# Attention operands issued in another order, and attention outputs stored as float32 and split where they are used

## The chip, the core and the metric

The kernel runs on one core of one Trainium2 chip. The metric is the time of one execution on the device in microseconds (us), the median of several runs. One core has five engines with queues of their own that run in order: TensorE (PE: matmuls, with its weight loads shown as PEld), VectorE (DVE), ScalarE (ACT), GpSimd (POOL) and SyncE (SP). In this kernel SP issues nearly all transfers between HBM and the on-chip memory (DMAs), which 16 DMA engines then carry out. Matmul results land in PSUM, in banks of 128x512 float32; VectorE and ScalarE read them from there.

## What is computed

One layer of a streaming encoder, 1024 positions of width 1024, in float32. Cut to the part around the change:

```python
h = rms_norm(x1, g_mix)
qa, ka, va, qb, kb, vb, ga, gb = split(h @ w_in)
oa = chunk_band_attention(norm(qa), norm(ka), va, rel_bias)
ob = diff_attention(rotary(norm(qb)), rotary(norm(kb)), vb, lam)
y  = sigmoid(ga) * (oa @ w_up_a) + sigmoid(gb) * (ob @ w_up_b)
x2 = x1 + y @ w_out
```

Attention A has 8 heads of 64: each query sees its own chunk of 64 positions and the 8 before it, with a learned bias by distance. Attention B has 4 heads, each with two softmax maps whose difference is applied. In front of this lies a gated feed-forward layer, behind it another and a last norm; the change touches neither.

## The kernel before

**Precision.** Every product is made of three: an operand is split into a high part (float32 rounded to `float32r`, a copy on ScalarE) and a low part (operand minus high part, a subtraction on VectorE), and `mm3` adds high x high, high x low and low x high. Weights are loaded raw (`w`), then split into `wh` (L211) and `wl` (L215). Three raw buffers and six split pairs circulate: a raw buffer is loaded again once its low part has been made.

**Order.** The program is written as one stream of PE instructions. Work of the other engines that follows a product is put into a *chain* (`pe.chain`): a list of steps, each with a delay in ns on a clock that counts PE's matmuls (`Lag.now`). A step is emitted when that clock has passed it, or at once when `settle` is called for one of the chain's keys. So the delays set where a step stands in its engine's queue, and no more; whether data are there is settled by semaphores when it runs. Tiles come from rings (`pe.tile(..., bufs)`): a ring of 2 gives the same memory again at every second call.

**Projections beside attention.** `filler` is a generator that makes the products of `h @ w_in`, one 128x512 result in eight steps of three matmuls. `steps(n)` draws n of them. Queries and keys are normed, transposed, split and stored (`qk_evac`), values split and stored (`v_evac`, L1218, staging ring `stg` of 2), gates stored (`g_evac`, L1228). Seven values' results are made ahead of attention A by `steps(7 * 8)`; the rest of the projections fills PE between the attention's own products.

**Attention A** (`PairA`, `run_a`). 8 heads of 4 pairs of 128-query blocks. Pair i's scores are made while pair i-1 is transposed and pair i-2 multiplied with the values. `prefetch` issues SP's loads: a head's keys `uk` (four DMAs, L1237) and bias (four, L1595) by `load(h)`; its queries in two halves of 512 (`uq`, ring of 2, two DMAs each, L1250) by `load_q(h, half)`; its values `uv` (L1300) by `load_v(h)`. Every second pair the 64x512 output is complete: it is added up in `olow`, split into `oT` (L1391, L1392), and both parts are stored to `o_d["a"]` (L1393).

**Attention B** (`ItemB`, `run_b`). 4 heads of 8 blocks. The normed output of a block is transposed, split into the two parts of `oT` (L1528, L1529), and after four blocks stored to `o_d["b"]` (L1532).

**Up-projection.** For each of two column halves c and each tile t of 128 positions there is a product "a" and a product "b" of 12 matmuls, "a" one tile ahead; `load_o` has loaded both parts of the attention's output for a tile, 512 KB in pieces of 512 bytes (L1632). The gates of a tile (`load_gates`, L1645, ring `xn` of 2 and one place more) go through a sigmoid (L1686) and are multiplied with the two products out of PSUM (L1691); the sum `y` (L1695) is transposed for the product with `w_out`, and frees the buffer for a later tile's gates. The product banks are a ring of 4 (`mm`) and one of 2 (`fill`), so six products can wait to be read.

Of the kernel before, what the change touches and what calls it, by code (L numbers as in the profile page):

```python
# [21 lines left out]
P = 128  # L22
# [232 lines left out]
def kernel(ctx, tc, io, out):  # L255
# [24 lines left out]
    qk_d = {n: dp.tile([P, 2, 4, S], F32, name=n + "_d") for n in ("qa", "ka", "qb", "kb")}  # L280
    v_d = {n: dp.tile([NT, P, 1024], F32, name=n + "_d") for n in ("va", "vb")}
    g_d = dp.tile([NT, P, 2, D], F32, name="g_d")
    o_d = {n: dp.tile([P, 2, 4, S], F32, name="o" + n + "_d") for n in "ab"}

    rope_d = dp.tile([P, 4 * NT * ROT], F32, name="rope_d")
    EW = 768
# [990 lines left out]
    class PairA:  # L1277
# [29 lines left out]
        def prefetch(self):  # L1307
            h, b = self.h, self.b
            self.load(h)
            self.load_q(h, b // 4)  # L1310
            self.load_v(h)
            if b == 2:
                self.load(h + 1)
            if b == 6:
                self.load_v(h + 1)
            if b % 4 == 2:
                self.load_q(h + b // 4, (b // 4 + 1) % 2)

        def score(self, i):
            sp = pools["sp"]  # L1320
# [41 lines left out]
        def values(self):  # L1362
            h, b = self.h, self.b
            v = self.v[h]
            pe.settle(self.ph)
            if b % 4 == 0:
                self.po[h, b // 4] = banks["o"]()
            po = self.po[h, b // 4]

            terms = [[], []]  # L1370
            for kb in range(self.k0, b + 2):
                at = [i for i, (_, k0, nk, _) in enumerate(self.p) if k0 <= kb < k0 + nk]
                for part in (self.ph, self.pl):
                    rhs = part[:, kb - self.k0, at[0] : at[-1] + 1, :]
                    terms[len(at) - 1].append((kb, at[0] + b % 4, at[-1] + 1 + b % 4, rhs))
            one, both = terms
            terms = both[:1] + one + both[1:]
            for i, (kb, q0, q1, rhs) in enumerate(terms):
                pe.matmul(
                    po[:, q0 * P : q1 * P], v[:, kb, :], rhs.rearrange("p a q -> p (a q)"),  # L1380
                    start=(i == 0), stop=(i == len(terms) - 1),
                )
            if b % 4 == 2:

                oT = pe.tile(ap, [P, 2, 512], F32R, "oT", 1)
                low = sp_tile([P, 512], "olow", 1)
                pe.chain(
                    (po, oT, low),
                    (340, lambda: nc.scalar.copy(low[:HD], po[HD:])),
                    (600, lambda: nc.vector.tensor_tensor(low[:HD], po[:HD], low[:HD], op=ALU.add)),  # L1390
                    (1090, lambda: nc.scalar.copy(oT[:HD, 0], low[:HD])),  # L1391
                    (1300, lambda: nc.vector.tensor_tensor(oT[:HD, 1], low[:HD], oT[:HD, 0].bitcast(F32), op=ALU.subtract)),  # L1392
                    (800, lambda: nc.sync.dma_start(  # L1393
                        o_d["a"][(h % 2) * HD : (h % 2 + 1) * HD, :, h // 2, (b - 2) * P : (b + 2) * P],
                        oT[:HD].bitcast(F32),
                    )),
                )

    def sp_tile(shape, tag, bufs):
        return pe.tile(pools["sp"], shape, F32, tag, bufs)  # L1400

    class ItemB:
# [114 lines left out]
        def finish(self):  # L1517
            h, b = self.h, self.b
            pe.settle(self.on)
            pt = banks["t"]()  # L1520
            pe.transpose(pt[:, :P], self.on, ident)
            if b % 4 == 3:
                self.oT[h, b // 4] = pe.tile(ap, [P, 2, 512], F32R, "oT", 1)
            oT = self.oT[h, b // 4]
            qs = slice((b % 4) * P, (b % 4 + 1) * P)
            pe.chain(
                (pt, self.on, oT),
                (88, lambda: nc.scalar.activation(oT[:, 0, qs], pt[:, :P], AF.Copy, scale=gsub)),  # L1528
                (350, lambda: nc.vector.scalar_tensor_tensor(  # L1529
                    oT[:, 1, qs], pt[:, :P], gsub, oT[:, 0, qs].bitcast(F32), op0=ALU.mult, op1=ALU.subtract  # L1530
                )),
                *([(420, lambda: nc.sync.dma_start(o_d["b"][:, :, h, b * P : (b + 4) * P], oT.bitcast(F32)))]  # L1532
                  if b % 4 == 0 else []),
            )

    def run_a(pairs):
# [67 lines left out]
    with tc.tile_pool(name="sa", bufs=1, reuse_waits="tile") as sp:  # L1604
        pools["sp"] = sp
        PairA.load(0)
        PairA.load_q(0, 0)
        steps(7 * 8)
        pe.poll(all=True)
        psum_stage("pp3", s=(1024, 1), t=(512, 3), o=(512, 1))  # L1610
        run_a([PairA(h, b) for h in range(8) for b in range(0, NT, 2)])
        pe.poll(all=True)
# [16 lines left out]
        oT["b", t] = fp.tile([P, 2, 4, P], F32R, name="ob", tag=f"e{t}")  # L1629

    def load_o(n, t):
        nc.sync.dma_start(  # L1632
            oT[n, t].bitcast(F32).rearrange("p a u s -> p (a u) s"),
            o_d[n][:, :, :, t * P : (t + 1) * P].rearrange("p a u s -> p (a u) s"),
        )

    gates, g2 = {}, []
# [6 lines left out]
                gates[c, t] = pe.tile(fp, [P, 2, 512], F32, "xn", 2)  # L1644
            nc.sync.dma_start(gates[c, t], g_d[t, :, :, c * 512 : (c + 1) * 512])  # L1645

    for t in range(4):
        load_o("a", t)
    load_gates(0, 0)
    for t in range(4):  # L1650
        load_o("b", t)
    for _ in filler:
        pass
    load_gates(0, 1)
# [6 lines left out]
    up = {}  # L1661

    def product(n, c, t):
        ps = up[n, c, t] = bank()
        o = oT[n, t]
        first = base_up + 4 * c + (0 if n == "a" else 2)
# [140 lines left out]
```

## Time and profile before

| | |
|---|---|
| median of 3 runs | 2191.67 us (2190.38 to 2193.26) |
| the profiled execution | 2190.83 us, span from first to last instruction 2189.1 us |
| PE busy | 2132.0 us, 97% of the span |
| VectorE, ScalarE, GpSimd busy | 1423.0, 861.7, 871.2 us |
| mean granted TensorE clock | 0.993 |
| DMA | 305.66 MB, mean 140 GB/s |
| attention A, attention B, up-projection begin at about | 822, 1012, 1340 us |

A busy PE says little about where time is lost; the waits do. A timeline row gives the start in us from the span's start, the length, the engine, the line and the instruction, and in brackets the idle time ahead of it and what ended that. For SP, several issues in a row are merged ("x4"), and their length includes time in which SP could not issue the next. The granted clock is the share of full speed at which PE was allowed to run in a stretch; its two levels are 2.4 GHz (1.00) and 1.2 GHz (0.50).

### The profile page before, as it was taken

To read this page: it belongs to the slowest core of one execution; us is meant where nothing else is said; L and a number is where in the kernel's file an instruction comes from. 1 tells how busy PE (TensorE), PEld (TensorE's weight loads), DVE (VectorE), ACT (ScalarE), POOL (GpSimd) and SP (SyncE) were. 2 spreads that over 40 slices of the span, in tenths; PEclk is the share of its full clock that TensorE was granted. 3 is DMA by queue.
4 is the path that set the end of the run, shared out by engine and by line. 5 is a ranking of instruction groups with operands and counts; after the bars stand their busy time and mean duration, and the time that the engine had idled before them with its cause. 6 is when DMAs were issued, how large, how long until landed. Compare 5 with 4: busy or idle time off the path is not lost.

```text
span 2189.1 us, 27974 instructions
## 1 busy us (share of the span) xinstructions
PE 2132.0 (97%) x10112; PEld 1777.7 (81%) x10112; DVE 1423.0 (65%) x2013; ACT 861.7 (39%) x1491; POOL 871.2 (40%) x775
## 2 busy tenths in 40 slices
PE   7999999999999998999999999899999999999998
PEld 6788888888877887887888888788788888888886
DVE  7767666677995435775666663433866566668698
ACT  5333223244334324664555553322433323235432
POOL 3645554453675314552111110000464544527375
PEclk9999999999999999999999999999999999999999
DMA  5234333376323456656543537632223333355531
GB/s 159 74 98 137 102 116 94 110 262 239 126 87 140 126 170 168 195 152 181 177 137 126 169 116 227 220 97 104 64 68 115 101 116 101 113 186 215 202 116 77
DMA packets 267602, 305.66 MB, mean 140 GB/s; under 512 B 17456, under 2 KB 177480, under 8 KB 267464
## 3 DMA queue, kind: packets, MB, share of 16 engines
q1 hardware_dynamic: 267320, 303.35, 43.4%
q8 instruction: 80, 1.31, 0.3%
q14 instruction: 58, 0.48, 0.1%
q0 software_dynamic: 144, 0.52, 0.1%
HBM read 210.21 MB, written 94.40 MB: 139 GB/s over the span
## 4 chain that ended last, share of the span: by engine, by line
PE 57%; DVE 5%; POOL 2%; DMA 2%; issue 2%; SPq 1%; ACT 1%; POOLq 0%; DVEq 0%; ACTq 0%
PE fill L90 28%; PE mm L90 20%; PE t L95 3%; PE s L90 3%; PE t L90 2%; DVE wl L215 2%; PE o L90 2%; SPq L1632 1%; POOL x L834 1%; DVE xTh L792 1%; DVE x L834 1%; DMA uq<-qa_d 0%; DMA xn<-g_d 0%; DVE acc L834 0%; POOL S L598 0%
## 5 line engine op out<-in xcount | busy, mean ns | idle before, releaser
L211 ACT CAST wh<-w 128x1024 fp32r<-128x1024 f32 (+1 forms) x228 | 201.3, 900 | 392.5 <-PE mm L90 130.1
L90 PE MATMUL fill<-wh,xTh 128*128 128x512 f32 x824 | 328.1, 405 | 3.4 <-DVE xTh L792 2.9
L215 DVE TENSOR_TENSOR wl<-w,wh 128x1024 fp32r<-128x1024 f32 (+1 forms) x227 | 293.7, 1308 | 37.2 <-ACT wh L211 36.5
L90 PE MATMUL fill<-wh,xTl 128*128 128x512 f32 x816 | 315.1, 393 | 0.0
L90 PE MATMUL fill<-wl,xTh 128*128 128x512 f32 x752 | 296.1, 394 | 0.0
L90 PE MATMUL mm<-xTl,wh 128*128 128x512 f32 (+1 forms) x572 | 220.4, 385 | 2.4 <-DVE xTl L616 1.8
L90 PE MATMUL mm<-xTh,wh 128*128 128x512 f32 (+1 forms) x572 | 221.1, 386 | 0.2 <-ACT xTh L450 0.2
L90 PE MATMUL mm<-xTh,wl 128*128 128x512 f32 (+1 forms) x572 | 220.1, 385 | 0.0
L90 PE MATMUL mm<-S,wh 128*128 128x512 f32 x640 | 197.0, 389 | 0.0
L90 PEld LDWEIGHTS fill<-wh,xTl 128*128 128x128 f32 x816 | 153.8, 189 | 33.2
L90 PEld LDWEIGHTS fill<-wh,xTh 128*128 128x128 f32 x824 | 155.5, 189 | 31.2 <-DVE xTh L792 3.3
L90 PEld LDWEIGHTS fill<-wl,xTh 128*128 128x128 f32 x752 | 142.3, 189 | 23.0
L90 PEld LDWEIGHTS mm<-S,wh 128*128 128x128 f32 x640 | 120.2, 188 | 24.9
L215 DVE TENSOR_TENSOR wl<-tw,wh 128x1024 fp32r<-128x1024 f32 x80 | 123.5, 1544 | 9.3 <-ACT wh L211 9.3
L90 PEld LDWEIGHTS mm<-xTl,wh 128*128 128x128 f32 x572 | 108.3, 189 | 24.5 <-DVE xTl L616 2.2
L457 POOL TENSOR_SCALAR rs<-ss 128x8 f32<-128x8 f32 (+1 forms) x56 | 11.5, 206 | 290.3 <-ACT xn L477 204.6
L90 PE MATMUL mm<-wh,xTh 128*128 128x512 f32 x376 | 126.6, 390 | 0.0
L90 PEld LDWEIGHTS mm<-xTh,wh 128*128 128x128 f32 x572 | 108.4, 189 | 21.6 <-ACT xTh L450 0.7
L90 PEld LDWEIGHTS mm<-xTh,wl 128*128 128x128 f32 x572 | 108.3, 189 | 21.2 <-POOL wl L215 0.2
L90 PE MATMUL mm<-S,wl 128*128 128x512 f32 x320 | 124.5, 389 | 0.0
L90 PE MATMUL mm<-wh,xTl 128*128 128x512 f32 x360 | 121.3, 389 | 0.0
L337 POOL TENSOR_TENSOR tw<-w,w 128x512 f32<-128x512 f32 x40 | 54.7, 1369 | 148.0 <-DVE wl L215 116.1
(259 smaller groups left out, 4846.5 us busy)
## 6 DMA issues: line engine op xcount, KB each, us to landing
w<-in_w_ffn_gu SPq DMA_DIRECT2D x88, 512.0 KB, 4.3
raw<-hq_d SPq DMA_DIRECT2D x70, 512.0 KB, 3.9
hq_d<-xn SPq DMA_DIRECT2D x98, 256.0 KB, 4.5
w<-in_w_ffn_down SPq DMA_DIRECT2D x44, 512.0 KB, 6.1
w<-in_w_in SPq DMA_DIRECT2D x40, 512.0 KB, 4.1
hq_d<-x SPq DMA_DIRECT2D x42, 256.0 KB, 4.2
x_d<-x SPq DMA_DIRECT2D x16, 512.0 KB, 3.2
uq<-qa_d SPq DMA_DIRECT2D x32, 256.0 KB, 5.1
```

Of the source, the lines that this page charges most:

```text
L90: self.nc.tensor.matmul(ps, lhs, rhs, **flags)
L95: self.nc.tensor.transpose(ps, x, ident)
L211: self.nc.scalar.copy(h, w)
L215: (lo_engine or self.nc.vector).tensor_tensor(l, w, h.bitcast(F32), op=ALU.subtract)
L337: nc.gpsimd.tensor_tensor(t[:, :512], u0, g0, op=ALU.subtract)
L457: nc.gpsimd.tensor_scalar(r, ss, 1.0 / n, EPS, op0=ALU.mult, op1=ALU.add)
L792: nc.vector.tensor_tensor(t[:, 1], raw, t[:, 0].bitcast(F32), op=ALU.subtract)
L834: return lambda: engine.tensor_tensor(to, by if by is not None else to, what, op=ALU.add)
L1632: nc.sync.dma_start(oT[n, t].bitcast(F32).rearrange("p a u s -> p (a u) s"), o_d[n][:, :, :, t * P : (t + 1) * P].rearrange("p a u s -> p ...
```

## The change

Three things are altered.

1. Ahead of attention A, the second half of head 0's queries and head 1's keys and bias are loaded after 16 of the 56 filler steps, not in the first pairs. Head 0's values are loaded at the second pair.
2. In `prefetch`, the next half head's queries are loaded ahead of the next head's keys and bias, and ahead of its values.
3. Attention outputs are stored as float32, not as two parts, in a layout by tile (`[P, NT, 4, P]`, so that what the up-projection loads for a tile is one run of 2 KB in each partition). `load_o` loads a tile into the place of its low part, and a chain splits it there: a copy on ScalarE into the high part, then a subtraction on VectorE in place. `product` settles that chain ahead of its first matmul. The loads for tiles 0 to 3 come in the order in which the products take them.

```diff
--- before.py
+++ after.py
@@ -280,7 +280,7 @@
     qk_d = {n: dp.tile([P, 2, 4, S], F32, name=n + "_d") for n in ("qa", "ka", "qb", "kb")}
     v_d = {n: dp.tile([NT, P, 1024], F32, name=n + "_d") for n in ("va", "vb")}
     g_d = dp.tile([NT, P, 2, D], F32, name="g_d")
-    o_d = {n: dp.tile([P, 2, 4, S], F32, name="o" + n + "_d") for n in "ab"}
+    o_d = {n: dp.tile([P, NT, 4, P], F32, name="o" + n + "_d") for n in "ab"}
 
     rope_d = dp.tile([P, 4 * NT * ROT], F32, name="rope_d")
     EW = 768
@@ -1308,13 +1308,14 @@
             h, b = self.h, self.b
             self.load(h)
             self.load_q(h, b // 4)
-            self.load_v(h)
+            if b % 4 == 2:
+                self.load_q(h + b // 4, (b // 4 + 1) % 2)
+            if b > 0:
+                self.load_v(h)
             if b == 2:
                 self.load(h + 1)
             if b == 6:
                 self.load_v(h + 1)
-            if b % 4 == 2:
-                self.load_q(h + b // 4, (b // 4 + 1) % 2)
 
         def score(self, i):
             sp = pools["sp"]
@@ -1382,17 +1383,15 @@
                 )
             if b % 4 == 2:
 
-                oT = pe.tile(ap, [P, 2, 512], F32R, "oT", 1)
-                low = sp_tile([P, 512], "olow", 1)
+                low = sp_tile([P, 512], "olow", 2)
+                t0 = b - 2
                 pe.chain(
-                    (po, oT, low),
+                    (po, low),
                     (340, lambda: nc.scalar.copy(low[:HD], po[HD:])),
                     (600, lambda: nc.vector.tensor_tensor(low[:HD], po[:HD], low[:HD], op=ALU.add)),
-                    (1090, lambda: nc.scalar.copy(oT[:HD, 0], low[:HD])),
-                    (1300, lambda: nc.vector.tensor_tensor(oT[:HD, 1], low[:HD], oT[:HD, 0].bitcast(F32), op=ALU.subtract)),
-                    (800, lambda: nc.sync.dma_start(
-                        o_d["a"][(h % 2) * HD : (h % 2 + 1) * HD, :, h // 2, (b - 2) * P : (b + 2) * P],
-                        oT[:HD].bitcast(F32),
+                    (1300, lambda: nc.sync.dma_start(
+                        o_d["a"][(h % 2) * HD : (h % 2 + 1) * HD, t0 : t0 + 4, h // 2, :],
+                        low[:HD].rearrange("p (t s) -> p t s", s=P),
                     )),
                 )
 
@@ -1520,17 +1519,15 @@
             pt = banks["t"]()
             pe.transpose(pt[:, :P], self.on, ident)
             if b % 4 == 3:
-                self.oT[h, b // 4] = pe.tile(ap, [P, 2, 512], F32R, "oT", 1)
+                self.oT[h, b // 4] = pe.tile(ap, [P, 512], F32, "oT", 2)
             oT = self.oT[h, b // 4]
             qs = slice((b % 4) * P, (b % 4 + 1) * P)
             pe.chain(
                 (pt, self.on, oT),
-                (88, lambda: nc.scalar.activation(oT[:, 0, qs], pt[:, :P], AF.Copy, scale=gsub)),
-                (350, lambda: nc.vector.scalar_tensor_tensor(
-                    oT[:, 1, qs], pt[:, :P], gsub, oT[:, 0, qs].bitcast(F32), op0=ALU.mult, op1=ALU.subtract
-                )),
-                *([(420, lambda: nc.sync.dma_start(o_d["b"][:, :, h, b * P : (b + 4) * P], oT.bitcast(F32)))]
-                  if b % 4 == 0 else []),
+                (88, lambda: nc.scalar.activation(oT[:, qs], pt[:, :P], AF.Copy, scale=gsub)),
+                *([(420, lambda: nc.sync.dma_start(
+                    o_d["b"][:, b : b + 4, h, :], oT.rearrange("p (t s) -> p t s", s=P)
+                ))] if b % 4 == 0 else []),
             )
 
     def run_a(pairs):
@@ -1605,7 +1602,10 @@
         pools["sp"] = sp
         PairA.load(0)
         PairA.load_q(0, 0)
-        steps(7 * 8)
+        steps(2 * 8)
+        PairA.load_q(0, 1)
+        PairA.load(1)
+        steps(5 * 8)
         pe.poll(all=True)
         psum_stage("pp3", s=(1024, 1), t=(512, 3), o=(512, 1))
         run_a([PairA(h, b) for h in range(8) for b in range(0, NT, 2)])
@@ -1629,9 +1629,15 @@
         oT["b", t] = fp.tile([P, 2, 4, P], F32R, name="ob", tag=f"e{t}")
 
     def load_o(n, t):
-        nc.sync.dma_start(
-            oT[n, t].bitcast(F32).rearrange("p a u s -> p (a u) s"),
-            o_d[n][:, :, :, t * P : (t + 1) * P].rearrange("p a u s -> p (a u) s"),
+
+        o = oT[n, t]
+        nc.sync.dma_start(o[:, 1].bitcast(F32), o_d[n][:, t])
+
+        need = 6300 if (n, t) == ("a", 0) else 9000 + 2720 * (2 * t - 1 if n == "a" else 2 * t + 2)
+        pe.chain(
+            (("o", n, t),),
+            (need - (15000 if t >= 4 else 0), lambda: nc.scalar.copy(o[:, 0], o[:, 1].bitcast(F32))),
+            (700, lambda: nc.vector.tensor_tensor(o[:, 1], o[:, 1].bitcast(F32), o[:, 0].bitcast(F32), op=ALU.subtract)),
         )
 
     gates, g2 = {}, []
@@ -1644,11 +1650,11 @@
                 gates[c, t] = pe.tile(fp, [P, 2, 512], F32, "xn", 2)
             nc.sync.dma_start(gates[c, t], g_d[t, :, :, c * 512 : (c + 1) * 512])
 
-    for t in range(4):
-        load_o("a", t)
+    for n, t in (("a", 0), ("a", 1), ("b", 0), ("a", 2)):
+        load_o(n, t)
     load_gates(0, 0)
-    for t in range(4):
-        load_o("b", t)
+    for n, t in (("b", 1), ("a", 3), ("b", 2), ("b", 3)):
+        load_o(n, t)
     for _ in filler:
         pass
     load_gates(0, 1)
@@ -1661,6 +1667,7 @@
     up = {}
 
     def product(n, c, t):
+        pe.settle(("o", n, t))
         ps = up[n, c, t] = bank()
         o = oT[n, t]
         first = base_up + 4 * c + (0 if n == "a" else 2)
```

**SP's queue from the first queries of attention A on, head 0** (`uq` queries, `uk` keys, `uv` values, `w_...` raw projection weights, `va_d` the stored values). Before:

```order
L1250 DMA uq<-qa_d 64x2x512 x2
L1218 DMA va_d<-stg 128x1024 x6
L174 DMA w_6383<-in_w_in 128x2x512
L174 DMA w_6402<-in_w_in 128x2x512
L1218 DMA va_d<-stg 128x1024
L174 DMA w_6410<-in_w_in 128x2x512
L174 DMA w_6416<-in_w_in 128x2x512
L1300 DMA uv<-va_d 128x8x128
L1237 DMA uk<-ka_d 64x512 x4
L1595 DMA bias<-e_d 32x576 x4
L1250 DMA uq<-qa_d 64x2x512 x2
L1300 DMA uv<-va_d 128x8x128
```

The same stretch of the changed kernel:

```order
L1250 DMA uq<-qa_d 64x2x512 x2
L1218 DMA va_d<-stg 128x1024
L1250 DMA uq<-qa_d 64x2x512 x2
L1237 DMA uk<-ka_d 64x512 x4
L1592 DMA bias<-e_d 32x576 x4
L1218 DMA va_d<-stg 128x1024 x5
L174 DMA w_6399<-in_w_in 128x2x512
L174 DMA w_6418<-in_w_in 128x2x512
L1218 DMA va_d<-stg 128x1024
L174 DMA w_6426<-in_w_in 128x2x512
L174 DMA w_6432<-in_w_in 128x2x512
L1300 DMA uv<-va_d 128x8x128
```

The second half's queries, and the next head's keys and bias, have moved from behind the values' load to behind the second store of values.

**SP's queue in head 5 of attention A**, at its second pair. Before:

```order
L1197 DMA kb_d<-stg 128x4x128 x2
L174 DMA w_8304<-in_w_in 128x2x512
L174 DMA w_8357<-in_w_in 128x2x512
L1237 DMA uk<-ka_d 64x512 x4
L1595 DMA bias<-e_d 32x576 x4
L1250 DMA uq<-qa_d 64x2x512 x2
L174 DMA w_8409<-in_w_in 128x2x512
```

The same stretch of the changed kernel:

```order
L1197 DMA kb_d<-stg 128x4x128 x2
L174 DMA w_8277<-in_w_in 128x2x512
L174 DMA w_8330<-in_w_in 128x2x512
L1250 DMA uq<-qa_d 64x2x512 x2
L1237 DMA uk<-ka_d 64x512 x4
L1592 DMA bias<-e_d 32x576 x4
L174 DMA w_8382<-in_w_in 128x2x512
```

The queries have passed the keys and the bias; the two weight loads still stand in front.

**VectorE's queue from the end of the projections into the up-projection** (`wl` low halves of weights, the fourth of them that of the fourth "a" up weight; L1698 multiplies a gate with a product; L1640 is the new subtraction). In the kernel before, only the rows without `oa` and `ob` are there. The changed kernel:

```order
L1640 TENSOR_TENSOR oa<-oa 128x512
L215 TENSOR_TENSOR wl<-w_11624,wh 128x1024
L1640 TENSOR_TENSOR oa<-oa 128x512
L215 TENSOR_TENSOR wl<-w_11666,wh 128x1024
L1640 TENSOR_TENSOR ob<-ob 128x512
L215 TENSOR_TENSOR wl<-w_11717,wh 128x1024
L1640 TENSOR_TENSOR oa<-oa 128x512
L215 TENSOR_TENSOR wl<-w_12225,wh 128x1024
L1698 TENSOR_TENSOR xn<-fill,xn 128x512
L1640 TENSOR_TENSOR ob<-ob 128x512
L1698 TENSOR_TENSOR xn<-mm,xn 128x512
L1702 TENSOR_TENSOR sg<-xn 128x512
```

The subtractions stand between the weights' low halves and the gate products; that of "b" tile 1 comes after the fourth low half and the first gate product. On ScalarE the new copies stand in the same way between the weights' high halves and the sigmoids.

## Rows read from the trace of the kernel before

**Rows 1.** Page part 1: busy us (share of the span) and instructions of each engine.

```profile
PE 2132.0 (97%) x10112; PEld 1777.7 (81%) x10112; DVE 1423.0 (65%) x2013; ACT 861.7 (39%) x1491; POOL 871.2 (40%) x775
```

**Rows 2.** Waits of PE: for what; us in total, times, longest us.

```profile
PE s L90 <- DMA uq<-qa_d: 10.6, 2, 6.4
...
PE mm L90 <- DVE xn L1691: 6.9, 1, 6.9
...
PE t L95 <- DVE p L1472: 1.2, 1, 1.2
...
PE t L95 <- DVE sg L1695: 0.6, 1, 0.6
```

**Rows 3.** Timeline of PE: start us, us, instruction, [idle before <-releaser].

```profile
840.22 1.51 PE L90 MATMUL s<-uk,uq 128*128 128x512 f32 x4 [6.35 <-DMA uq<-qa_d]
...
994.08 1.51 PE L90 MATMUL s<-uk,uq 128*128 128x512 f32 x4 [4.21 <-DMA uq<-qa_d]
...
1378.88 0.80 PE L90 MATMUL mm<-wh,oa 128*128 128x512 f32 x1 [6.92 <-DVE xn L1691]
```

**Rows 4.** Stretches: us, busy us PE, PEld, DVE, ACT, POOL, granted PE clock, DMA share, GB/s.

```profile
840.20:846.50 6.30, 6.28 (x21) 5.42 (x22) 1.55 (x4) 1.97 (x4) 0.80 (x1) 0.52 0.42 92
994.10:1000.30 6.20, 6.20 (x22) 5.32 (x23) 1.55 (x4) 1.91 (x4) 0.80 (x1) 0.54 0.50 177
1378.90:1382.30 3.40, 3.40 (x8) 2.66 (x9) 3.33 (x6) 0.63 (x1) 0.00 (x0) 0.52 0.22 69
...
1340.00:1372.00 32.00, 31.32 (x143) 25.31 (x141) 9.51 (x13) 8.05 (x9) 0.78 (x1) 1.00 1.06 313
```

**Rows 5.** Timeline of SP's queue, attention A, head 0.

```profile
828.13 0.37 SPq L1300 DMA_DIRECT2D uv<-va_d  x1
828.54 2.50 SPq L1237 DMA_DIRECT2D uk<-ka_d  x4
831.09 3.46 SPq L1595 DMA_DIRECT2D bias<-e_d  x4
834.70 1.18 SPq L1250 DMA_DIRECT2D uq<-qa_d  x2
```

**Rows 6.** DMA issues by line: count, KB each, median us from issue to landing.

```profile
uv<-va_d SPq DMA_DIRECT2D x8, 512.0 KB, 5.6
```

**Rows 7.** Timeline of SP's queue, attention A, head 5.

```profile
982.16 2.78 SPq L1237 DMA_DIRECT2D uk<-ka_d  x4
...
987.40 1.18 SPq L1250 DMA_DIRECT2D uq<-qa_d  x2
```

**Rows 8.** Timeline of ScalarE (ACT), up-projection.

```profile
1351.95 1.05 ACT L211 CAST wh<-w 128x1024 fp32r<-128x1024 f32 x1 [8.12 <-DMA w<-in_w_up_a]
...
1356.94 0.59 ACT L450 CAST xTh<-t 128x512 fp32r<-128x512 f32 x1 [2.59 <-PE t L95]
...
1377.05 1.06 ACT L1686 ACTIVATE xn<-xn 128x1024 f32<-128x1024 f32 x1 [14.05 <-DMA xn<-g_d]
```

**Rows 9.** Timeline of VectorE (DVE), end of the projections and up-projection.

```profile
1336.78 2.59 DVE L215 TENSOR_TENSOR wl<-w,wh 128x1024 fp32r<-128x1024 f32 x2 [9.88 <-ACT wh L211]
...
1355.50 0.69 DVE L1695 TENSOR_TENSOR sg<-xn 128x512 f32<-128x512 f32 x1
```

**Rows 10.** Timeline of SP's queue around the up-projection's start.

```profile
1327.65 6.58 SPq L1632 DMA_DIRECT2D oa<-oa_d  x4
...
1335.99 7.64 SPq L1632 DMA_DIRECT2D ob<-ob_d  x4
...
1368.29 0.73 SPq L1645 DMA_DIRECT2D xn<-g_d  x1
```

**Rows 11.** Timeline of SP's queue: a gate store from 128x512.

```profile
1323.99 0.32 SPq L1228 DMA_DIRECT2D g_d<-qn  x1
```

**Rows 12.** Timeline of PE: the first product with "b" tile 1.

```profile
1350.45 0.39 PE L90 MATMUL mm<-wh,ob 128*128 128x512 f32 x1
```

**Rows 13.** Stretch of one head in attention A; columns as in Rows 4.

```profile
850.19:879.50 29.31, 29.31 (x175) 25.48 (x174) 19.96 (x50) 16.54 (x39) 16.74 (x32) 1.00 0.57 149
```

## The prediction, made before the changed kernel was run

> **What bounds the kernel now.** First the page's busy times: TensorE (PE) has 97% of the span [rows 1], so only the time in which it stands still, or runs at a lower clock, is to be had. The list of what PE waited for says how much that is: two waits for the queries of attention A make 10.6 us, one for a product of the gates 6.9, one for a transposed gate product 0.6; no wait for VectorE in attention is above 1.2 [rows 2]. PE's timeline places the three long ones [rows 3]: 6.35 us in head 0 (first scores of block 4), 4.21 in head 5 (the same place), 6.92 in the up-projection, where a bank is not yet read out. The table by stretches adds what follows each: the granted clock is 0.52, 0.54 and 0.52 for 6.30, 6.20 and 3.40 us, close to the lower of the two levels [rows 4]. The stages between run without a stop. PE's instructions and their order are the same in both kernels; only their starts can move.
>
> **The change, part by part.**
>
> *A. Queries and keys of head 0.* Half 1 of head 0's queries is issued at 834.70, behind the values' load (828.13), which waits for the last store of va, and behind four key and four bias loads [rows 5]; the data come at 840.2, when PE has stood since 833.9 [rows 3]. Now these ten loads go out right behind va's second store, six stores sooner. Worth: 6.35 + 6.30 x (1 - 0.52) = 6.35 + 3.02 = 9.4 us. What is late next? The values: still issued at about 828.1, and the median of their loads is 5.6 us [rows 6], so they land at 833.7. Their first product stands behind four score matmuls (1.51 us at the low clock, half that at the high one [rows 3]), so PE wants them at about 834.6. That leaves 0.9 us, and the load now has the queue to itself, so I take 0, with a bound of 1 us. The price of the move: six stores of va stand behind ten more DMAs, which take SP 2.50 + 3.46 + 1.18 = 7.1 us [rows 5]. Their two staging buffers come free later and ScalarE waits for one; behind it stand only evacuations, and each bank is filled again four groups later (two tags of two banks): 0.
>
> *B. Every later half head.* The two query loads move ahead of four key and four bias loads: in head 5 from 987.40 to 982.16 [rows 7], 5.2 us against a wait of 4.21. Two weight loads still go out before them; what they may leave of the wait I put at 0, with a bound of 1 us. Worth: 4.21 + 6.20 x (1 - 0.54) = 4.21 + 2.85 = 7.1 us. Keys and bias go out 1.2 us later, for a head that starts three block pairs later: 0.
>
> *C. The up-projection.* PE waits there for a bank that the product with gate (0,3) has not read; VectorE waits for the sigmoid, ScalarE for the gate's load, 14.05 us [rows 8]. The gate's buffer was free when gate (0,0) had been added up, at 1355.50 + 0.69 = 1356.2 [rows 9], but SP issued the load at 1368.29 [rows 10]: it was busy with attention outputs, 6.58 us for four "a" tiles and 7.64 for four "b", so 1.65 to 1.9 each and 26 to 31 us for the 16. Each moves 1024 pieces of 512 bytes; now it moves half the bytes in 128 pieces of 2 KB. A DMA of that shape (a gate store, 128x512) takes SP 0.32 us [rows 11]; if time goes by bytes instead, half of 1.9 is 0.95. So all 16 take between 5 and 15 us, and SP is 11 to 26 us earlier; I take the nearer row, the same shape. Then gate (0,3) goes out by 1356.2, and even with the 8.8 us that it took here (1368.29 to the sigmoid's start at 1377.05) it is in by 1365.0, through the sigmoid by 1366.1 and multiplied by 1366.8, where PE stopped only at 1372.0. Worth: 6.92 + 3.40 x 0.48 = 8.55. The 0.6 at the first transposed gate product goes too, since the fourth "a" up weight, for which ScalarE waited 8.12 us [rows 8], is also issued sooner. Together 9.2 us.
>
> *D. The split moves.* Removed in attention: 16 casts and 16 subtractions in A, 32 subtractions in B. PE waits little for these engines there (1.2 us at most [rows 2]): a gain of 0 to 1, and I take 0. Added in the up-projection: 16 casts of 128x512 on ScalarE and 16 subtractions on VectorE; the nearest rows are 0.59 [rows 8] and 0.69 us [rows 9], 9.4 and 11.0 us beside an ScalarE busy 8.05 us in 32 and a VectorE busy 9.51 [rows 4]. They cost nothing as long as each ends before its product; without that cover, 16 x 1.28 = 20 us. The tightest is "b" 1: its split stands behind the high half of the fourth "a" up weight on ScalarE, its subtraction behind the low half. That weight's load can go out when the first raw buffer is read, at 1336.78 + 1.3 = 1338.1 [rows 9]. With 5.6 us [rows 6] it is in at 1343.7, with the 8.8 of C at 1346.9. Then cast 1.05, subtraction 1.3, gate product 0.69, split 0.69: done at 1347.4 or 1350.6, and PE wants it at 1350.45 [rows 12]. I take 0 (DMA has less to move now), with a bound of 1 us.
>
> *E. Stores.* Half the bytes, but in pieces of 512 bytes where attention had 2 KB. Only the first "b" load waits for one: it holds SP until the last store has landed. By the 5.6 us of rows 6, the largest near row, it leaves at about 1333 and is wanted two products (5.4 us) before "b" 1, at 1345: 0.
>
> **Sum.** 9.4 + 7.1 + 9.2 = 25.7 us. The profiled execution took 2190.8 us (span 2189.1), 0.8 below the median of the runs, 2191.67. So 2165.1 for that execution and **2166.0** for the median.
>
> **Rivals.**
> 1. *All three waits go*, as above: 2166, from 2165 to 2169 by the bounds in A to D.
> 2. *One wait comes back in another place.* In C: if the queue is not what held the gate, or the splits queue up behind the up weight, up to 9.2 us stay: 2175. For it: the DMA engines are full in that stretch (share 1.06 [rows 4]), so SP may have been slow because they were. Against: half the bytes halve that too. In A or B, values or queries 1 to 4 us late: 2167 to 2172. A page speaks for the first. The Trainium skill (DMA: Bandwidth & Descriptors, "Issuing engines are not separate DMA queues") says that the time a sequencer takes to initiate a DMA is usually small against the DMA itself. By that rule fewer pieces would free nothing on SP, and the time would be 2175; 6.58 us of SP for four loads [rows 10] speaks against it.
> 3. *The waits only shift.* VectorE or GpSimd becomes the bound of attention A once PE no longer stops, and 2188 to 2192 comes out. Against: a head's length without a wait runs with PE busy 29.31 of 29.31 us, VectorE 19.96 and GpSimd 16.74 [rows 13].
> 4. *Slower: split on demand.* ScalarE and VectorE take their instructions in order. If a cast waits for its load, or stands behind a late sigmoid, each split ends after its product is due: PE waits 16 times 1.28 us, 20 us, and, stopping before every product, stays at the lower clock for the pass: 192 matmuls of 0.425 us (3.40 us for 8 [rows 4]) instead of half that cost 41 more. With A and B gained, 2191.7 - 16.5 + 61 = 2236. It decides where splits end later than their products by more than the 0 to 3 us that D leaves; with a third of the products late it is 2195. Against: the loads start at 1327.65 [rows 10], and the first split is due four products before "b" 1, about 1339.6.
>
> **How the numbers follow.** Case 1 has 0.73, case 2 0.19, case 3 0.03, case 4 0.05. A measurement of this kernel can tell about 0.2%, 4.4 us, from no change; cases 1 and 2 lie beyond that, case 3 within it. Faster 0.92, same 0.03, slower 0.05. The range takes in case 1 with its bounds, 4 us more for small gains in attention that I put at 0, and case 2: 2161 to 2176, leaving out cases 3 and 4.
>
> **What would show it.** Right: no wait of PE for uq and none for the gate products above 1 us; the granted clock at 1.00 through attention A and the up-projection; the gate load (0,3) on SP right behind the first gate sum instead of 12 us after it; the 16 output loads in under 15 us of SP. Wrong: a wait for a split (oa, ob) or for uv in PE's list, a clock below 1 in these stages, or the same 10.6 us under another name.

## The result, and the profile after

The changed kernel takes 2164.22 us (median of 4 runs, 2162.68 to 2164.97) against 2191.18 for the kernel before on the same chip (4 runs, 2190.38 to 2193.26): a ratio of 0.9881 (95% interval 0.9869 to 0.9893), 27.0 us less. Forecast were 2166.0 and a range of 2161 to 2176. The time lies in the range, and what happened is the forecast's likeliest case: all three waits are gone. It is 0.8 us below the 2165 to 2169 that this case had by its own bounds, in the part of the range that was kept for small gains in attention. The profiled execution has a span of 2163.2 us, 25.9 less than before's 2189.1; the forecast's sum was 25.7.

PE has the same 10112 instructions. Of the 25.9 us, 19.6 are time in which it stood still (57.1 before, 37.5 now), and 6.3 are busy time, since fewer of its matmuls run at the lower clock (compare [rows 1]):

```profile
PE 2125.7 (98%) x10112; PEld 1773.4 (82%) x10112; DVE 1413.9 (65%) x1981; ACT 860.9 (40%) x1491; POOL 866.1 (40%) x775
```

32 VectorE instructions are gone: the 48 subtractions in attention less the 16 added in the up-projection. On ScalarE as many casts came as went.

What PE waits for between 815 and 1520 us (columns as in [rows 2]). The 10.6 for `uq`, the 6.9 for the gate product, the 0.6 for `sg` and the 1.2 for `p` are all gone, and no `oa`, `ob` or `uv` has come in. The 1.0 for `xTl` is not new: the kernel before has it at 1529.27, outside of this stretch.

```profile
PE s L90 <- DVE m L1337: 1.3, 1, 1.3
PE t L95 <- DVE xTl L451: 1.0, 1, 1.0
PE t L90 <- DVE pTl L1274: 0.7, 1, 0.7
PE o L90 <- DVE pTl L1274: 0.3, 1, 0.3
PE o L90 <- ACT pTh L1273: 0.2, 1, 0.2
PE s L90 <- DVE stg L1215: 0.2, 1, 0.2
```

PE's timeline at the places of [rows 3]: block 4's scores in head 0 and in head 5, and the first product of the up-projection. None has a bracket, so none was waited for, and four score matmuls take 0.80 us where they took 1.51 at the low clock:

```profile
834.43 0.80 PE L90 MATMUL s<-uk,uq 128*128 128x512 f32 x4
...
981.10 0.80 PE L90 MATMUL s<-uk,uq 128*128 128x512 f32 x4
...
1322.02 0.39 PE L90 MATMUL fill<-wh,oa 128*128 128x512 f32 x1
```

The stretches of the changed kernel (columns as in [rows 4]): attention A up to 1012 us, the rest of both attentions up to 1320, then a place in the feed-forward layer behind the up-projection, of which more below, and last the up-projection's start. The granted clock is at 1.00 in attention and at the up-projection's start, where [rows 4] had 0.52 to 0.54. The table ahead of the prediction lets attention B begin at about 1012 us, which is too early: attention A's last sum runs at 1074.59 in the kernel before and at 1058.72 in the changed one (rows under D).

```profile
822.00:1012.00 190.00, 188.48 (x1102) 162.62 (x1101) 126.25 (x312) 107.01 (x243) 94.76 (x176) 1.00 0.66 179
1012.00:1320.00 308.00, 306.79 (x1673) 262.65 (x1672) 181.99 (x421) 163.51 (x412) 35.78 (x76) 1.00 0.43 135
...
1528.90:1536.00 7.10, 7.07 (x28) 5.64 (x29) 6.94 (x16) 2.88 (x8) 0.00 (x0) 0.76 0.11 39
1320.00:1360.00 40.00, 40.00 (x186) 33.10 (x185) 26.13 (x39) 19.43 (x28) 0.78 (x1) 1.00 0.63 223
```

SP's queue in head 0 answers to [rows 5]. Queries, keys and bias go out 31 to 39 us sooner; the values go out when they did:

```profile
796.20 1.58 SPq L1250 DMA_DIRECT2D uq<-qa_d  x2
797.82 2.55 SPq L1237 DMA_DIRECT2D uk<-ka_d  x4
800.42 2.59 SPq L1592 DMA_DIRECT2D bias<-e_d  x4
...
828.64 0.37 SPq L1300 DMA_DIRECT2D uv<-va_d  x1
```

SP's queue at the up-projection answers to [rows 10]. Shown are the first and the last of the attention outputs' loads and gate (0,3), that is column half 0 and tile 3:

```profile
1309.52 1.42 SPq L1634 DMA_DIRECT2D oa<-oa_d  x2
...
1311.62 0.32 SPq L1634 DMA_DIRECT2D ob<-ob_d  x1
...
1328.90 0.32 SPq L1634 DMA_DIRECT2D ob<-ob_d  x1
...
1332.33 0.85 SPq L1651 DMA_DIRECT2D xn<-g_d  x1
```

The 16 loads have rows of 0.32 to 0.71 us each and 8.0 in all, where four of them took 6.58 and 7.64 before. VectorE's rows there: "b" 1's subtraction, and the first sum of the gates, which frees the buffer for gate (0,3):

```profile
1330.03 0.68 DVE L1640 TENSOR_TENSOR ob<-ob 128x512 fp32r<-128x512 f32 x1
...
1331.34 0.69 DVE L1702 TENSOR_TENSOR sg<-xn 128x512 f32<-128x512 f32 x1
```

The sum ends at 1332.0 and the gate's load leaves 0.3 us later, not 12.

To see where the 25.9 us come from, the span is divided at two points on PE: its first score of attention A, and its first product of the up-projection (1322.02 above; before: 1339.58).

| us | before | after | difference | forecast |
|---|---|---|---|---|
| up to the first score | 822.3 | 822.8 | +0.5 | 0 |
| both attentions | 517.3 | 499.2 | -18.1 | -16.5 (A, B) |
| up-projection to the end | 849.5 | 841.2 | -8.3 | -9.2 (C) |

The sum is right to 0.2 us, but with 1.6 more in attention and 0.9 less behind it; the experiments look for both. The 0.5 ahead of the first score is no more than what the executions differ by: it stands between 822.2 and 822.8 in the twelve that were profiled.

### The profile page after: what moved, and what is told of

It reads as the page before. It is cut to its first block, busy times and chain, and to the rows that moved or that the text cites. A ratio compares the mean times of both kernels' runs of the same rounds, so it can differ in the third digit from the quotient of the medians.

```text
span 2163.2 us, 27972 instructions
## 1 busy us (share of the span) xinstructions
PE 2125.7 (98%) x10112; PEld 1773.4 (82%) x10112; DVE 1413.9 (65%) x1981; ACT 860.9 (40%) x1491; POOL 866.1 (40%) x775
## 4 chain that ended last, share of the span: by engine, by line
PE 89%; DVE 5%; POOL 3%; issue 1%; ACT 1%; DMA 1%; POOLq 0%; DVEq 0%; ACTq 0%
PE mm L90 38%; PE fill L90 37%; PE t L90 5%; PE t L95 4%; PE s L90 3%; PE o L90 2%; DVE wl L215 1%; POOL S L598 1%; POOL S L600 1%; POOL S L599 1%; DMA w<-in_w_ffn_gu 1%; POOL x L834 0%; DVE xTl L616 0%; DVE xn L484 0%; DVE xTl L451 0%
```

## The experiments

Each kernel ran on one chip beside the kernel before; ratios are against that. The middle columns are the stages of the table above, from each kernel's profiled execution. The attention column moves also where an edit does not touch it (517.3 before, 511.1 and 510.9 in e4 and e5); the parts on A and B below say why.

| kernel | both attentions | rest | span | median us | ratio (95%) |
|---|---|---|---|---|---|
| e1: part 1 alone | 505.5 | 849.6 | 2177.5 | 2180.6 | 0.9961 (0.9949 to 0.9972) |
| e2: part 2 alone | 503.1 | 851.0 | 2176.9 | 2179.8 | 0.9959 (0.9946 to 0.9972) |
| e3: part 3 alone | 512.2 | 841.2 | 2176.0 | 2176.7 | 0.9944 (0.9932 to 0.9956) |
| e4: before, outputs laid out by tile | 511.1 | 839.5 | 2173.3 | 2179.4 | 0.9951 (0.9939 to 0.9963) |
| e5: before, four loads moved | 510.9 | 840.1 | 2173.7 | 2178.2 | 0.9950 (0.9937 to 0.9964) |
| e6: after, splits on demand | 499.0 | 849.1 | 2170.7 | 2173.9 | 0.9927 (0.9914 to 0.9939) |
| e7: after, old layout | 498.9 | 839.5 | 2160.9 | 2162.9 | 0.9879 (0.9865 to 0.9892) |
| e8: e4 with parts 1 and 2 | 500.9 | 839.5 | 2163.2 | 2164.9 | 0.9887 (0.9873 to 0.9902) |
| e9: after, again | 498.9 | 839.4 | 2160.5 | 2162.5 | 0.9877 (0.9860 to 0.9893) |
| e10: e7 again | 499.2 | 841.1 | 2162.9 | 2164.1 | 0.9883 (0.9869 to 0.9898) |

**e1, the early loads of head 0 alone.** The kernel before with

```diff
-            self.load_v(h)
+            if b > 0:
+                self.load_v(h)
...
-        steps(7 * 8)
+        steps(2 * 8)
+        PairA.load_q(0, 1)
+        PairA.load(1)
+        steps(5 * 8)
```

> The kernel before, with the first part of the change alone: head 0's second half of queries and head 1's keys and bias are loaded after 16 filler steps, and head 0's values at the second pair. Theory (what is lost is the wait and the lower clock behind it): PE's wait of 6.35 us in head 0 goes and with it the 3.0 us at half clock, the other two long waits stay as they are, 9.4 us less, a ratio of 0.9957. Rival 1 (only the wait counts): 6.4 us less. Rival 2 (the values are late next, or six delayed stores of values hold PE): a new wait for uv or stg in head 0 of 1 to 6 us, 3 to 8 us less.

Head 0 has no wait for queries, and none for values or the staging buffers has come in its place. Head 5 still waits; PE's timeline there, and the stretch behind it (columns as in [rows 4]):

```profile
983.57 0.87 PE L90 MATMUL s<-uk,uq 128*128 128x512 f32 x4 [2.93 <-DMA uq<-qa_d]
```

```profile
983.50:989.50 6.00, 5.93 (x27) 5.21 (x28) 2.19 (x5) 2.28 (x5) 0.80 (x1) 0.72 0.76 268
```

Attention is 11.8 us shorter. Head 5 cost 7.1 before and costs 2.93 + 6.00 x (1 - 0.72) = 4.6 here, through no part of the edit; so head 0's share is 11.8 - 2.5 = 9.3. The median fell by 7.7 us, between the 9.4 of the expectation and the 6.4 of its first rival: the rows tell the two apart, the time alone does not.

**e2, queries ahead of keys and bias, alone.** The kernel before with these lines moved up:

```diff
+            if b % 4 == 2:
+                self.load_q(h + b // 4, (b // 4 + 1) % 2)
             self.load_v(h)
...
-            if b % 4 == 2:
-                self.load_q(h + b // 4, (b // 4 + 1) % 2)
```

> The kernel before, with the second part alone: the next half head's queries ahead of the next head's keys, bias and values. Theory for head 5: its wait of 4.21 us goes with 2.9 us of half clock, 7.1 us less. In head 0 the queries then leave SP right behind the values' load, at about 828.6 in place of 834.7, and land some 5.4 us later at 834.0, when PE wants them at 833.9. So if the delay on SP is all there is, head 0 is cured as well, a wait of 1 us or less is left and the time falls by 15 to 16.5 us: then the first part of the change adds nothing to the second. Rival (each part cures its own head): head 0 still waits 3 us or more with the clock low after it, 7 to 9 us less in all.

Head 5's wait is gone. In head 0 this edit alone leaves little, for there too the queries now pass four key and four bias loads; PE's timeline:

```profile
836.29 0.87 PE L90 MATMUL s<-uk,uq 128*128 128x512 f32 x4 [1.48 <-DMA uq<-qa_d]
```

That lies between the two outcomes that were expected, 1 us or less and 3 us or more. After 1.48 us of waiting the clock stayed at 1.00. So parts 1 and 2 overlap: attention is 14.2 us shorter by part 2 alone and 11.8 by part 1 alone, and e8, with both, is only 2.2 below e2. The median fell by 8.4 us where the trace shows 12.2 less span; e2's six runs spread from 2175.8 to 2183.3, and the time alone would not have settled it.

**e3, the outputs alone.** The changed kernel with parts 1 and 2 undone.

> The changed kernel with the loads of attention A as before: only the third part (outputs stored as float32 by tile, split in the up-projection). Theory: the waits for queries stay at 6.35 and 4.21 us, the wait for gate (0,3) of 6.92 us, its 3.4 us at half clock and the 0.65 us wait go, 9.2 us less, a ratio of 0.9958. Rival (the gate's load was late for another reason than SP's queue, or the added splits cost): 0 to 4 us less.

The waits for queries stay, though shorter than before (5.54 and 2.66 us); the gate's wait, the one for `sg` and the one for `p` are gone. The rest is 8.3 us shorter, as in the changed kernel. Attention is 5.1 us shorter, which was not expected: the shorter waits (A and B below) and the moved split (D) make it up.

**e4, the layout without the format.** Both parts are still made in attention and stored, 512 KB a load, but by tile, so that a load is 128 pieces of 4 KB where it was 1024 of 512 bytes; a store is issued as two, one for each part (not shown here):

```diff
-    o_d = {n: dp.tile([P, 2, 4, S], F32, name="o" + n + "_d") for n in "ab"}
+    o_d = {n: dp.tile([P, NT, 2, 4, P], F32, name="o" + n + "_d") for n in "ab"}
...
-        nc.sync.dma_start(
-            oT[n, t].bitcast(F32).rearrange("p a u s -> p (a u) s"),
-            o_d[n][:, :, :, t * P : (t + 1) * P].rearrange("p a u s -> p (a u) s"),
-        )
+        nc.sync.dma_start(oT[n, t].bitcast(F32), o_d[n][:, t])
```

> The kernel before with the outputs still split in attention and stored as two parts, but in a layout by tile, so that a load of the up-projection is 512 KB in 128 pieces of 4 KB in place of 1024 of 512 bytes; each store is issued as two (one per part), 24 more. Nothing is split in the up-projection. Theory (SP's time for a load goes with its number of pieces): 0.3 to 0.6 us of SP per load in place of 1.65 to 1.9, the gate's load goes out by 1357, its wait goes, 9 us less, as much as with float32 outputs: the halved bytes and the moved split are not what pays. Rival (SP's time goes with the bytes, because the DMA engines are full): 1.5 us or more per load, the wait stays at 5 us or more, 0 to 3 us less.

SP's queue has the same bytes as [rows 10] in a third of the time:

```profile
1321.83 2.07 SPq L1634 DMA_DIRECT2D oa<-oa_d  x4
...
1324.70 2.35 SPq L1634 DMA_DIRECT2D ob<-ob_d  x4
```

The gate's wait is gone. The loads themselves are no faster: the medians from issue to landing are 7.8 ("a") and 10.0 us ("b"), 8.2 and 8.5 before. So the pieces set what a load costs SP, and SP's time is what the gate waited for.

**e5, the same loads at another place in the queue.** Nothing in the kernel before is changed but that tiles 6 and 7 are loaded behind gates (0,3) and (0,4):

```diff
-    for t in range(4, NT):
+    for t in range(4, 6):
...
             product("b", c, t)
+            if c == 0 and t in (1, 2):
+                for n in "ab":
+                    load_o(n, t + 5)
```

> The kernel before, with the loads of the last four attention outputs (a and b of tiles 6 and 7) moved behind the loads of gates (0,3) and (0,4) in SP's queue; the same DMAs with the same pieces and bytes. Theory (the gate's load stood in SP's queue behind loads that nobody needed yet): gate (0,3) leaves SP at about 1358 in place of 1368.29, PE's wait of 6.92 us and the half clock after it go, 7 to 9 us less with no change of layout or format. Rival (the DMA engines were full, and the gate's data come as late as before): the wait stays at 4 us or more, 0 to 3 us less. Third outcome: the moved loads come late themselves, a wait for oa or ob of tile 6.

Gate (0,3) leaves SP here, 19 us after the first product against 29 before:

```profile
1352.81 0.75 SPq L1645 DMA_DIRECT2D xn<-g_d  x1
```

PE has no wait for it, and the rest is 9.4 us shorter, with all the pieces and bytes of before. The median fell by 12.0 us, more than the 7 to 9 expected; in the profiled execution 6.4 us come from attention, which this edit does not touch. The 9.4 settle the cause of term C: it is the gate's place in SP's queue.

**e6, the cover of the splits taken away.** The changed kernel with each split emitted only when its product settles it:

```diff
-            (need - (15000 if t >= 4 else 0), lambda: nc.scalar.copy(o[:, 0], o[:, 1].bitcast(F32))),
+            (1e9, lambda: nc.scalar.copy(o[:, 0], o[:, 1].bitcast(F32))),
```

> The changed kernel with every output split emitted only when its product is about to be issued, not 3 to 6 us of PE work ahead. This is the cover under which the splits were costed at nothing. If each of the 16 products waits for its cast and subtraction: 16 times 1.28 us, and the lower clock for the pass, 20 to 61 us more than the changed kernel. If it is enough that ScalarE and VectorE reach the split while PE is still in the products emitted before it: waits of 1 us or less here and there, 0 to 5 us more.

Five products wait, all of them "b"; PE's list of waits:

```profile
PE mm L90 <- ACT ob L1639: 3.7, 3, 1.3
PE fill L90 <- ACT ob L1639: 2.9, 2, 1.7
```

Why "b" waits is seen on ScalarE, VectorE and PE at the longest of them. The cast of `ob` stands behind the sigmoid (second row; the gate's tile is called `gain` here), which stands behind a copy that waits for PE's own transposition of `y`; the cast of the next `oa` comes right behind it, a whole product ahead of its use. VectorE's subtraction for `ob` follows the cast:

```profile
1338.36 0.58 ACT L450 CAST xTh<-t 128x512 fp32r<-128x512 f32 x1 [8.06 <-PE t L95]
1338.85 1.06 ACT L1693 ACTIVATE gain<-gain 128x1024 f32<-128x1024 f32 x1
1339.80 0.61 ACT L1639 CAST ob<-ob 128x512 fp32r<-128x512 f32 x1
1340.31 0.62 ACT L1639 CAST oa<-oa 128x512 fp32r<-128x512 f32 x1
```

```profile
1340.44 0.69 DVE L1640 TENSOR_TENSOR ob<-ob 128x512 fp32r<-128x512 f32 x1 [3.37 <-ACT ob L1639]
```

```profile
1338.40 0.39 PE L90 MATMUL mm<-wh,oa 128*128 128x512 f32 x1
1340.46 0.50 PE L90 MATMUL fill<-wh,ob 128*128 128x512 f32 x1 [1.68 <-ACT ob L1639]
1340.80 0.40 PE L90 MATMUL fill<-wl,ob 128*128 128x512 f32 x1
1341.19 0.73 PE L90 MATMUL fill<-wh,ob 128*128 128x512 f32 x2
```

The clock stayed at 1.00. The rest is 9.7 us longer than in e9: 6.6 of waits, some 0.4 behind each stop, which makes 2.0, and about 1 that the rows do not explain. The 0.4 are lost over the first matmuls, which start 0.34 to 0.39 us apart and not 0.23; the third of them is the first to need the low part, and it starts when the subtraction has ended, at 1341.13. Neither expected outcome came: the loss is above the 0 to 5 us of the one and below the 20 to 61 of the other.

**e7, float32 in the old layout.** The changed kernel, but `o_d` is `[P, 4, S]`, so that a load has the same 256 KB in 512 pieces of 512 bytes (the stores follow):

```diff
-        nc.sync.dma_start(o[:, 1].bitcast(F32), o_d[n][:, t])
+        nc.sync.dma_start(o[:, 1].bitcast(F32), o_d[n][:, :, t * P : (t + 1) * P])
```

> The changed kernel with float32 outputs in the old layout, so that a load is 256 KB in 512 pieces of 512 bytes in place of 128 of 2 KB. By the number of pieces (or by the bytes) SP's time for a load is half of that before, 0.8 to 0.95 us, 15 us for 16: gate (0,3) still leaves SP some 10 us earlier than before, and the time is the changed kernel's within 1 us. Rival (the layout is needed): the wait for the gate comes back with 2 us or more, the time is 3 to 9 us above the changed kernel's.

SP takes 0.5 to 1.9 us a load, 14.6 in all. Two of its rows:

```profile
1308.81 2.26 SPq L1634 DMA_DIRECT2D oa<-oa_d  x2
...
1326.35 1.92 SPq L1634 DMA_DIRECT2D oa<-oa_d  x1
```

That is still early enough for the gate: no wait, and the time of the changed kernel.

**e8, everything but the format.** e4 with parts 1 and 2; the splits stay in attention.

> Both parts on the loads of attention A, and the layout by tile, but the outputs still split in attention and stored as two parts (as in the layout experiment): the change without its float32. Theory (the moved split gives back what VectorE held up at the seam between attention A and B): PE's wait of 1.2 us for the first transposes of B and some 0.3 us beside it are there again, from the first score to the up-projection 500.7 to 501.7 us in place of the changed kernel's 499.2, the up-projection as fast: 1.5 to 2.5 us above the changed kernel. Rival (the split's place is worth nothing): within 0.5 us of it and no such wait. It does not have the 16 copies and subtractions in the up-projection, so if those cost anything it gains that back there.

It is 2.4 us slower than e9 beside it (2164.90 against 2162.53; their runs don't overlap), and 2.0 of it are in attention: 500.9 against 498.9. One wait of [rows 2] is back:

```profile
1066.63 1.09 PE L95 MATMUL t<-ident,p 128*128 128x128 f32 x8 [1.23 <-DVE p L1473]
```

**e9 and e10, the changed kernel and e7 once more, side by side.**

> The changed kernel once more, beside the experiment without float32 on the same chip, so that the two can be set against each other: 25 to 28 us below the kernel before, and no wait above 1.5 us in attention A or the up-projection.

> Float32 outputs in the old layout once more, beside the changed kernel on the same chip: if the layout by tile is worth something, this is 1 us or more above the changed kernel; if fewer bytes are enough, the two are within 1 us.

e9 took 2162.5 and e10 2164.1; in the first runs it was 2164.2 and 2162.9. The order turned round, so the two layouts can't be told apart. In the profiled executions the slower of each pair is the one whose clock fell in front of the second feed-forward layer (C below). The fastest other version, e7 in its first runs, lies 1.3 us below the changed kernel, less than the 1.7 between the changed kernel's own two medians.

## Why the prediction was right, and where its terms were off

**What bounds the kernel.** Right: with PE's work unchanged, the time went by how long PE stood still and by the clock behind each stop.

**The sum, 25.7 us: measured 25.9, closer than its terms.** Attention gave 1.6 us more than forecast (D). The up-projection's start gave up to 10 where 9.2 were forecast (C), but 1.7 were lost again behind a wait that the change does not touch, and 0.5 ahead of the first score. In e9, the same kernel without that loss, the span is 2160.5. So the 0.2 is luck; that the time lies in the range is not.

**A, 9.4 us: measured 9.3** (e1, against the execution of before that the forecast read). Left alone, head 0 cost less in other kernels: in e3 a wait of 5.54 us and, by this row, 6.00 x (1 - 0.68) = 1.9 at the lower clock, 7.5 in all:

```profile
839.70:845.70 6.00, 5.98 (x27) 5.25 (x28) 2.04 (x5) 2.14 (x5) 0.81 (x1) 0.68 0.51 111
```

In e4 and e5 it was 7.6 and 7.1 (waits of 5.86 and 5.42 us, and a clock of 0.72 and 0.74 for 6.30). The values, feared late, were not: in the changed kernel they are issued at 828.64 and their first product runs at 835.07 without a wait. What the forecast missed is that its step B also reaches head 0: without A, only 1.48 us and some tenths would have been left there.

**B, 7.1 us: right for the execution that was read, and near the upper end of what comes up.** The same wait in kernels that leave head 5's order alone came out shorter, with and without a drop of the clock. PE's timeline and the stretch behind it in e3, and in e5, whose attention has the code of before:

```profile
991.00 1.51 PE L90 MATMUL s<-uk,uq 128*128 128x512 f32 x4 [2.66 <-DMA uq<-qa_d]
```

```profile
991.00:997.00 6.00, 6.00 (x19) 5.12 (x20) 1.56 (x4) 1.69 (x4) 0.80 (x1) 0.50 0.71 240
```

```profile
990.84 0.87 PE L90 MATMUL s<-uk,uq 128*128 128x512 f32 x4 [2.65 <-DMA uq<-qa_d]
```

```profile
990.80:997.00 6.20, 6.16 (x37) 5.46 (x38) 3.99 (x10) 3.65 (x8) 0.80 (x1) 1.00 0.81 283
```

With e1's 4.6, e4's 2.2, e3's 2.66 + 3.0 = 5.7 and e5's 2.65, term B lies between 2.2 and 7.1. The execution of before had the longest waits for queries of all that were profiled, in head 0 as in head 5. One profile of before can't show that a wait for a transfer varies so much; the forecast gave the term a bound of 1 us.

**C, 9.2 us: measured 9.4** (e5), 10.0 to 10.1 (e4, e7, e8 and e9) and 8.3 to 8.4 (the changed kernel, e3 and e10). The mechanism held at each step: the loads' 8.0 us of SP lie in the 5 to 15 of the forecast, the gate follows its buffer, the wait is gone. The 8.3 has a cause of its own. In front of the second feed-forward layer, at 1528.88, PE starts its transpositions after a wait of 1.83 us for VectorE, and in that execution the clock behind it was 0.76 for 7.10 us (the third row of the stretches above), 7.10 x 0.24 = 1.7 us. In e9 the same wait, 1.85, left it at 1.00, and the rest is 1.8 shorter:

```profile
1528.00:1536.00 8.00, 7.73 (x41) 6.26 (x41) 7.84 (x18) 3.72 (x10) 0.00 (x0) 1.00 0.09 34
```

The drop is there in e1, e2, e3 and e10 too, and in no other execution that was profiled; it lengthens the rest of e1 and e2, whose waits for the gate are a little shorter than before (5.88 and 6.59 us against 6.92).

**D, taken as 0: this is the term that was mis-sized.** Taking the splits out of attention was put at 0, with at most 1 us, and gave 1.7 to 2.0 (e8 against the changed kernel and e9). The forecast said that PE waits little for these engines there, and pointed at the wait of 1.2 for `p` without asking what VectorE did ahead of it. VectorE's timeline of the kernel before, where attention A ends and the first reduction of attention B (`mb`) follows:

```profile
1074.59 0.68 DVE L1390 TENSOR_TENSOR olow<-o,olow 64x512 f32<-64x512 f32 x1 [1.92 <-ACT olow L1389]
1075.96 0.68 DVE L1392 TENSOR_TENSOR oT<-olow,oT 64x512 fp32r<-64x512 f32 x1 [0.69 <-ACT oT L1391]
1076.66 0.11 DVE L1459 MEMSET s<- 64x64 f32 x1
```

And of the changed kernel:

```profile
1058.72 0.68 DVE L1391 TENSOR_TENSOR olow<-o,olow 64x512 f32<-64x512 f32 x1 [1.92 <-ACT olow L1390]
1059.41 0.11 DVE L1458 MEMSET s<- 64x64 f32 x1
```

From the sum's end to the next instruction it was 1.4 us (0.69 of waiting for the cast, 0.68 of subtraction); now it is 0. VectorE's chain to `p` starts that much sooner, and PE's 1.2 us go. Every profiled kernel that splits in attention has this wait (before, e1, e2, e4, e5, e8), and none of those that split later has it. Another 0.3 is in PE's waits for `pTl` and `pTh` (1.5 in all in e8, 1.2 in e9). The rest of the 2.0 is not explained; e8 also issues 24 more stores.

The cost of the 16 splits in the up-projection was 0, as taken. "b" 1, called the tightest, ends at 1330.7 and PE takes it at 1332.90: 2.2 us to spare, in the 0 to 3 of the forecast. The tightest was "b" 7: its subtraction ends at 1363.8, and PE takes it at 1365.2. But the price of losing that cover was set much too high: 61 us by rival 4, about 10 by e6. 11 of the 16 products don't wait there: the eight "a", whose cast comes a product ahead of its use, and "b" of tiles 0, 1 and 7; and waits of 1.7 us and less did not bring the clock down, so the 41 us for it were not paid.

**E, 0:** PE has no wait for `oa` or `ob`, so no store held up a load that PE needed.

**The rivals.** Nothing of the second came in. Its reason was that SP might be slow because the DMA engines were full; e4 moves the same bytes, whose landing got no faster, and SP needs a third of the time. The Trainium skill (DMA: Bandwidth & Descriptors, "Issuing engines are not separate DMA queues") says that the time to initiate a DMA is usually small against the DMA. In the kernel before it was 1.6 to 1.9 us against a landing of 8.2 to 8.5, about a fifth. The share is not what decides here: the next load stands behind the issue, and 16 of them took 30 us of SP. With 128 pieces it is 0.32 to 0.6 against 7.8 to 10.0 (e4), and there the rule fits. The third rival falls with attention A at a clock of 1.00 and no wait above 1.3.

## What to carry to other kernels

In a queue that issues loads in order, count what each load takes of the queue by its pieces, and look at who stands behind it: either fewer pieces (e4, e7) or another place in the queue (e5) cured this wait alone, and neither left any of it for the other. Where two edits are aimed at one wait, run each alone: part 1 brings 9.3 us alone, but only 2.2 once part 2 is in. And before a small wait is written off, read what the engine it waits for did just ahead of it; it may be the very instruction that the change removes.

## What the runs showed of the hardware that was not expected

- The time that SP takes to issue a load goes by its pieces more than by its bytes: 512 KB in 1024 pieces took 1.5 to 1.9 us as a mean of four, 512 KB in 128 pieces 0.32 to 0.59, 256 KB in 512 pieces 0.5 to 1.9, 256 KB in 128 pieces 0.32 to 0.71. The pieces do not fix it for a single load: those of 1024 took from 0.61 to 4.09 us (e5), and no row names what else SP waited for.
- Near the same length of wait, the clock falls in one execution and not in another: 2.65 us left it at 1.00, 2.66 brought it to 0.50 for 6 us; 1.83 brought it to 0.76 for 7.1 us in one execution, 1.85 left it alone in another. Over the twelve profiled executions this last wait (1.82 to 1.85 us) had the lower clock behind it in five, and one of 2.9 us in the first feed-forward layer, at about 643, in six. The eight waits of 4.2 to 6.9 us between 815 and 1520 us all brought it down.
- The kernels without a wait for queries or a gate also have closer runs: the changed kernel and e6 to e10 spread over 0.2 to 2.6 us in 4 or 5 runs each, e1 to e5 over 3.9 to 7.5 in 5 or 6, and the kernel before over 4.7 to 8.2 in 7 to 11 (2.9 in its first 4). The numbers of runs differ, and that the waits are the cause is not shown.
